# A row softmax on one core: the tail divides and stores ahead of the next maximum, and the whole-tile multiplies move to the even tiles

## The chip, the cores and the metric

One core of a Trainium2 chip runs the kernel. The metric is the device time of one execution in microseconds (us), lowest is best. A run's profile gives the span from the first to the last instruction; the device time is about 1.8 us longer.

## The reference

```python
# x: float32 (32, 512, 1024), temperature = 0.5
scaled = x / temperature
shifted = scaled - np.max(scaled, axis=-1, keepdims=True)
exp_x = np.exp(shifted)
return (exp_x / np.sum(exp_x, axis=-1, keepdims=True)).astype(np.float32)
```

There are 16,384 rows of 1,024 numbers, 67 MB in and 67 MB out.

## The kernel before

The rows are cut into 16 tiles (0 to 15) of 128 partitions with 8 rows each, 4 MB a tile. The kernel keeps six tile buffers (`BUFS`). The four outer tiles (0, 1, 14, 15) are worked in two groups of four rows, called 14a, 14b and so on below, the others in one group of eight.

```python
PASSES = [[4, 4]] * 2 + [[8]] * 12 + [[4, 4]] * 2
WHOLE = (3, 5, 7, 9, 11, 13)
ALIGNED = 3
BY_SP = 2
# ... cut: tiles, groups, dram() ...

def maximum(g):      # DVE: one reduction of the group, then bias = -scale * max
    ...
def exponential(g):  # ACT: one activation a row, exp(scale * x + bias), in place, with the row's sum
    ...
def divide(g):
    i, a, k = groups[g]
    _, sums, recip = small[g]
    nc.vector.reciprocal(recip, sums)
    if i in WHOLE:   # one multiplication for the tile
        xt = tiles[i][:, a : a + k, :]
        nc.vector.tensor_mul(xt, xt, recip.unsqueeze(2).to_broadcast([P, k, d]))
        return
    for b in range(k):  # or one a row
        nc.vector.tensor_scalar_mul(
            tiles[i][:, a + b, :], in0=tiles[i][:, a + b, :], scalar1=recip[:, b : b + 1]
        )

def store(g):        # when a tile's last group is divided; the next load waits for its buffer
    i, a, k = groups[g]
    if a + k == ROWS:
        queue = nc.scalar if i < len(PASSES) - BY_SP else nc.sync
        queue.dma_start(out=dram(of, i), in_=tiles[i])
        load()

for _ in range(BUFS):
    load()
for g in range(len(groups) + 1):
    if g < len(groups):
        maximum(g)
        exponential(g)
    if g > 0:
        divide(g - 1)
        store(g - 1)
    if g == ALIGNED:
        nc.vector.addr_align(128, offset=0, max_nops=0)
        nc.scalar.addr_align(128, offset=0, max_nops=0)
```

Loads go out on the queue of SyncE (SP), the stores of tiles 0 to 13 on that of ScalarE (ACT), those of 14 and 15 on SP's. In the trace they are the queues q1 and q10.

## Time and profile before

| | before |
|---|---|
| device time, first three runs | 318.0 us median (317.99 to 318.73) |
| span of the profiled run | 316.5 us |
| VectorE (DVE) busy | 250.8 us, 79% |
| ScalarE (ACT) busy | 148.2 us, 47% |
| moved by DMA | 134 MB, 433 GB/s from 40 to 280 us |

The page gives sums for the whole span, the windows view the same for chosen stretches, and the timeline the instructions in order, each with the idle time of its engine before it and what ended that in brackets. A DMA packet counts in the window of its start, so a share can be over 1 just behind a hole. The prediction below shows the lines that carry its argument. It also follows single packets: on a DMA engine that never pauses, each packet starts some 3 ns before the recorded end of the one in front, so one engine's packets can be followed through the trace, but for ties where two engines end within a nanosecond.

One more line of before is needed, from the view of everything that touches the output tensor (duration of issuing one in ns, then the times of the first and last issue): the stores on SP's queue.

```profile
L105 SPq DMA_DIRECT2D out_dram<-xt x2: 344/346/348, 291.4 to 303.6; - x2
```

### The profile page before, as it was taken

Reading aid. Unit: us, or ns where it says so; the run is one execution under the profiler, and the core shown is the slowest. Engines: PE = TensorE matmul, PEld = TensorE weight load, DVE = VectorE, ACT = ScalarE, POOL = GpSimd, SP = SyncE. Lnnn points to the kernel's source line nnn. Section 1 sums busy time; section 2 is a strip of 40 time slices with the busy share of each in tenths; the row PEclk is TensorE's granted clock in tenths of the full one; section 3 lists DMA queues with packets and bytes.
Section 4 is the critical chain, followed back from the end, with each engine's and each line's share of the span. In section 5 each row is a group of like instructions: output and inputs, shape, how many; then the busy total and the mean of one; then the engine's idle time right before and its main releaser. Section 6 shows DMA issues by size and latency. Waiting matters only on the chain.

```text
span 316.5 us, 534 instructions
## 1 busy us (share of the span) xinstructions
DVE 250.8 (79%) x146; ACT 148.2 (47%) x257; POOL 0.2 (0%) x4
## 2 busy tenths in 40 slices
DVE  0399999969989398994979859797697967999730
ACT  0176637681906429073380833709256092446600
POOL 0000000000000000000000000000000000000000
DMA  8999999999999999999999999999999999999996
GB/s 327 414 451 431 364 454 422 443 443 418 447 414 447 418 443 414 460 406 456 415 447 427 435 447 414 447 418 443 418 456 406 456 418 443 431 431 452 407 410 273
DMA packets 4613, 134.26 MB, mean 424 GB/s; under 512 B 512, under 2 KB 512, under 8 KB 512
## 3 DMA queue, kind: packets, MB, share of 16 engines
q1 hardware_dynamic: 2592, 75.50, 55.8%
q10 hardware_dynamic: 2016, 58.72, 43.0%
q14 instruction: 5, 0.04, 0.0%
HBM read 67.11 MB, written 67.11 MB: 424 GB/s over the span
## 4 chain that ended last, share of the span: by engine, by line
DVE 77%; another core or an unknown queue 11%; DMA 4%; ACT 3%; issue 1%; DVEq 0%; ACTq 0%
DVE top L70 43%; DVE xt L94 16%; DVE xt L97 16%; DMA xt<-in_x_dram 4%; ACT xt L79 3%; DVE recip L91 1%; DVE bias L73 1%; DVEq L154 0%; ACTq L154 0%
## 5 line engine op out<-in xcount | busy, mean ns | idle before, releaser
L79 ACT ACTIVATE xt<-xt,bias 128x1024 f32<-128x1024 f32 x128 | 145.2, 1135 | 139.2 <-DVE bias L73 121.8
L70 DVE TENSOR_REDUCE top<-xt 128x8 f32<-128x8192 f32 (+1 forms) x20 | 139.5, 6976 | 49.4 <-DMA xt<-in_x_dram 49.4
L97 DVE TENSOR_SCALAR xt<-xt,recip 128x1024 f32<-128x1024 f32 x80 | 54.3, 748 | 0.5
L94 DVE TENSOR_TENSOR xt<-xt,recip 128x8192 f32<-128x8192 f32 x6 | 52.1, 8692 | 0.2
L79 ACT ACTIVATION_READ_ACCUMULATOR xt<-xt,bias 128x1 f32 x128 | 23.8, 186 | 0.0
L79 ACT ACT_TABLE_LOAD x1 | 1.3, 1283 | 13.2 <-DMA xt<-in_x_dram 13.2
L91 DVE RECIPROCAL recip<-sums 128x8 f32<-128x8 f32 (+1 forms) x20 | 3.7, 185 | 2.0 <-ACT xt L79 2.0
L73 DVE TENSOR_SCALAR bias<-top 128x8 f32<-128x8 f32 (+1 forms) x20 | 3.4, 170 | 0.7
L140 POOL MEMSET const-bfloat16-1.0<- 128x1 bf16 x1 | 0.1, 101 | 0.0
L140 POOL MEMSET const-uint8-127<- 128x1 uint8 x1 | 0.1, 101 | 0.0
L140 POOL MEMSET const-float32-0.0<- 128x1 f32 x1 | 0.1, 98 | 0.2 <-issue 0.2
L140 POOL MEMSET const-float32-1.0<- 128x1 f32 x1 | 0.1, 98 | 0.0
## 6 DMA issues: line engine op xcount, KB each, us to landing
xt<-in_x_dram SPq DMA_DIRECT2D x16, 4096.0 KB, 50.4
out_dram<-xt ACTq DMA_DIRECT2D x14, 4096.0 KB, 28.8
out_dram<-xt SPq DMA_DIRECT2D x2, 4096.0 KB, 13.3
```

What stands on the lines that cost most here:

```text
L70: nc.vector.tensor_reduce(out=top, in_=tiles[i][:, a : a + k, :], axis=mybir.AxisListType.X, op=extreme)
L73: nc.vector.tensor_scalar_mul(bias, in0=top, scalar1=-scale)
L79: nc.scalar.activation(tiles[i][:, a + b, :], tiles[i][:, a + b, :], mybir.ActivationFunctionType.Exp, bias=bias[:, b : b + 1], scale=scal ...
L91: nc.vector.reciprocal(recip, sums)
L94: nc.vector.tensor_mul(xt, xt, recip.unsqueeze(2).to_broadcast([P, k, d]))
L97: nc.vector.tensor_scalar_mul(tiles[i][:, a + b, :], in0=tiles[i][:, a + b, :], scalar1=recip[:, b : b + 1])
L140: nc = _bacc.Bacc("TRN2", target_bir_lowering=False, num_devices=1)
```

## The change

Its intent: in the tail, where nothing is loaded any more, a tile should be divided and stored as soon as its exponentials are there, and not behind the maximum of the next tile. The other part turns the parity of the tiles that are multiplied whole (8.69 us instead of 5.39 in pieces), so that tile 13, the one ahead of the tail, is done in pieces.

```diff
-WHOLE = (3, 5, 7, 9, 11, 13)
+WHOLE = (2, 4, 6, 8, 10, 12)
 
 ALIGNED = 3
+
+ALONE = 14
@@
         for g in range(len(groups) + 1):
+
+            alone = g < len(groups) and groups[g][0] >= ALONE and groups[g][1] == 0
+            if g > 0 and alone:
+                divide(g - 1)
+                store(g - 1)
             if g < len(groups):
                 maximum(g)
                 exponential(g)
-            if g > 0:
+            if g > 0 and not alone:
                 divide(g - 1)
                 store(g - 1)
```

## The prediction

> **What bounds the kernel now.** I read the busy digits of the page first, then busy time by windows, then the waits, the timeline of VectorE (DVE) over the last 75 us, and last the single DMA packets of the trace. The page and the windows:
>
> ```profile
> DVE 250.8 (79%) x146; ACT 148.2 (47%) x257; POOL 0.2 (0%) x4
> ...
> DMA  8999999999999999999999999999999999999996
> ```
>
> ```profile
> core 0: us, DVE busy (x) ACT busy (x) POOL busy (x), PEclk, DMA share, GB/s
> ...
> 40.00:280.00 240.00, 202.83 (x99) 116.62 (x204) 0.00 (x0) 1.00 1.00 433
> 280.00:292.00 12.00, 11.86 (x15) 8.04 (x14) 0.00 (x0) 1.00 1.01 435
> 292.00:302.00 10.00, 8.05 (x10) 5.87 (x12) 0.00 (x0) 1.00 0.99 427
> 302.00:303.50 1.50, 1.50 (x3) 0.00 (x0) 0.00 (x0) 1.00 0.86 371
> 303.50:304.40 0.90, 0.10 (x1) 0.00 (x0) 0.00 (x0) 1.00 0.17 73
> ```
>
> The reader should see that DVE is idle for a fifth of the span, while the 16 DMA engines have share 1.00 and 433 GB/s from 40 to 280 us. Only one hole shows, at 303.5 to 304.4 us (share 0.17; a packet counts in the window of its start). So DMA is the bound, although the chain of waits puts 77% on DVE. The waits agree: it is DVE that waits for loads.
>
> ```profile
> DVE top L70 <- DMA xt<-in_x_dram: 49.4, 12, 13.2
> DVE recip L91 <- ACT xt L79: 2.0, 2, 1.8
> ```
>
> The tail of the timeline:
>
> ```profile
> 243.82 8.69 DVE L70 TENSOR_REDUCE top<-xt 128x8 f32<-128x8192 f32 x1 [1.63 <-DMA xt<-in_x_dram]
> ...
> 252.85 5.39 DVE L97 TENSOR_SCALAR xt<-xt,recip 128x1024 f32<-128x1024 f32 x8
> 263.19 4.42 DVE L70 TENSOR_REDUCE top<-xt 128x4 f32<-128x4096 f32 x1 [4.95 <-DMA xt<-in_x_dram]
> ...
> 267.95 8.69 DVE L94 TENSOR_TENSOR xt<-xt,recip 128x8192 f32<-128x8192 f32 x1
> 276.56 4.41 DVE L70 TENSOR_REDUCE top<-xt 128x4 f32<-128x4096 f32 x1
> ...
> 300.65 0.18 DVE L91 RECIPROCAL recip<-sums 128x4 f32<-128x4 f32 x1 [1.85 <-ACT xt L79]
> 300.86 2.74 DVE L97 TENSOR_SCALAR xt<-xt,recip 128x1024 f32<-128x1024 f32 x4
> ```
>
> Tile 13 was there from 243.8 us on, but its division waits behind the maximum of tile 14's first half, and that waits 4.95 us for load 14. In the timeline the store of tile 13 is issued at 276.7, of 14 at 291.4, of 15 at 303.6.
>
> The packets of the trace carry the verdict. Each of the 32 transfers is 128 packets of 32 KB, so 8 on each DMA engine, at 1.213 us each. An engine owes 256 packets, 310.5 us; the first starts at 1.76 us, so 312.3 us is the earliest end without any loss. The last packet ends at 315.26. At the seam between stores 14 and 15, twelve engines finish store 14 at 303.4 to 303.9 and stand still until 304.5, when the first packets of store 15 start there (0.84 us after its issue); averaged over 16 engines the hole costs 0.76 us. But two engines still have a packet of store 14 to do and finish it at 305.48 and 305.58; they pass into store 15 with no hole and end it at 315.16 and 315.26, the other fourteen at 314.2 to 314.4. So the end belongs to two late engines that never starve. They came late long before: around 35 us, when the first store starts, packets take 1.6 to 1.9 us, one 2.77, and without holes from there on nothing is made up.
>
> **What the Trainium skill says.** "HBM Reference", section "Specifications (TRN2)", says that a core streaming alone measures well above its share of the domain, about 425 GB/s, bounded by its 16 DMA engines; the 433 GB/s agree. "DMA: Bandwidth & Descriptors", section "Queues, rings and completion order", says that each DMA engine goes round-robin between the queues it has work for, packet by packet, and that sync's and scalar's queues lie on the same engines. The trace agrees: loads and stores each move about half of the 433. Thus a store that is issued earlier takes turns with the others and adds no bandwidth. The same page, section "Why a DMA increments its semaphore by 16 and not by 1", says that the engines of one DMA finish independently and only the full count means landed: hence the latest engine decides, as the ends at 314.2 and 315.26 show. "VectorE: DVE Perf Modes", section "The perf-mode tier table", has fp32 tensor_scalar at 2x and tensor_tensor at 1x; the trace has 5.39 us for a tile in eight pieces and 8.69 whole.
>
> **The change part by part.** (1) The parity. Six tiles are still multiplied whole, so DVE's sum stays 250.8 us. Stores of even tiles come up to 3.3 us (8.69 - 5.39) later, of odd ones earlier. In the middle DVE has 4.95 us to spare before each maximum after an eight-piece tile, and 1.6 after a whole one; with the parity turned these change places. The store queue doesn't run dry: store 1 ends its packets at 75.6, and store 2 goes from 66.2 to about 69.6. Only tile 2 pushes on DVE: its multiply ends at 60.8 + 8.7 = 69.5, not 66.2, while load 4 lands at 68.8, so the maximum of tile 4 starts 0.7 late, which the next slack of nearly 5 us takes up. Cost 0.
>
> (2) The tail, with durations from the timeline (maximum of 4 rows to its bias 4.44, four exponentials 4.6 until the sums are out, four multiplies 2.74, eight 5.39; some 0.2 from reciprocal to multiply). Tile 12, now whole: 252.85 + 8.69 = 261.54; its store goes from 258.3 to 261.6, behind store 11, which keeps that queue until 269.2. The exponentials of 13 end at 261.91, so its reciprocal at 261.95 and eight multiplies 262.2 to 267.6: store 13 at 267.6 instead of 276.7. Maximum 14a 267.5 to 271.9 (load 14 has been there since 263.2), exponentials to 276.8, maximum 14b beside them to 276.4, division 14a to 279.8. Now the second half must be divided ahead of maximum 15a, and DVE waits for the exponentials of 14b until 281.4 (1.6 us): division until 284.4, store 14 at 284.4 instead of 291.4. Maximum 15a from 284.3 (load 15 landed at 282.5), 15b from 288.8, exponentials of 15b until 298.2, last division 298.4 to 301.1: store 15 at 301.2 instead of 303.6. DVE's path gains 2.4 us: the 4.95 us wait for load 14 goes, about 0.4 of it comes back for 13's sums, and some 2 more for those of 14 and 15.
>
> (3) What becomes of that on DMA. Loads end at 280.9 as before. Store 12 keeps its queue until 285.3, 13 follows, 14 takes turns with 13 from about 286 on. All packets up to store 14 are the same work on engines that never pause, so it ends at about 303.5 on twelve engines, 305.6 on two, as before. Store 15 has packets ready at 301.2 + 0.84 = 302.0: the hole of 303.5 to 304.5 is closed. The twelve engines then end at 303.5 + 8 x 1.213 = 313.2, a microsecond sooner; the two late ones end at 305.58 + 9.70 = 315.28, as before. Sum: 2.4 us on DVE, 0.76 us of mean DMA idleness filled, near 0 at the end. From the last packet to the end of the span there are 1.2 us, and from span to time 1.8 (318.26 - 316.5); both stay.
>
> **The rivals.** First, the end follows the issue of store 15, as the chain of waits suggests: 318.0 - 2.4 = 315.6. Against it: between issue and end there is nothing for DMA to fill but the hole. Second, the late engines are chance of this profile, and others see the whole hole: 318.0 - 1.0 = 317.0. For it: one profile is one draw. Against it: the three timed runs are 317.99, 318.00 and 318.73. Without late engines the end would be 304.5 + 9.75 = 314.25, 1.0 us under the profiled one, about 317.25, and none of the runs is there. Third, a new wait makes it slower: late even stores empty the store queue, or tile 4's late maximum runs on to the end: at most +0.7, 318.7. Against it: 6 us of margin in the queue and the slack after tile 3. Fourth, instruction fetches (8 KB packets of 0.31 us on one engine, at 287 and 300 us) fall on the late engine: +0.3.
>
> **Range and chances.** I give six tenths to "late engines decide" (317.9), three tenths to the second rival or part of it (317.1), the rest to both sides: about 317.6 us. Range 316.5 to 318.6. Two per cent are 6.4 us; the largest gain that DMA allows is down to 312.3 + 1.2 + 1.8 = 315.3, 0.9%. So faster by over 2% has chance 0.01, within 0.98, slower 0.01.
>
> **What would show it.** Right: store 15 issued near 301.2, 14 near 284.4, 13 near 267.6; DMA share near 1 through 303 to 305 us; DVE's wait for loads down from 49.4 to about 44 (two of the twelve gone, 14's and 4's), its wait for ACT up from 2.0 to about 4.4; the last packets spread over 2 us, most at 313.2 and a few at about 315. Wrong: a last packet near 313.5 (the lateness isn't there or is made up), or a new hole before 300 us. An end above 319 us would mean that the store queue starved.

## The result, and the profile after

| | before | after |
|---|---|---|
| device time, median of 6 runs | 318.02 us (317.66 to 318.73) | 318.21 us (318.09 to 318.80) |
| span of the profiled run | 316.5 us | 316.3 us |
| last store issued | 303.6 us | 300.9 us |
| packets of 14 DMA engines end | 314.2 to 314.4 us | 313.0 to 313.6 us |
| packets of the two late ones end | 315.16, 315.26 us | 314.79, 315.07 us |

The ratio after to before is 1.0006, with a 95% interval from 0.9992 to 1.0019: the same time. Here and below a ratio is the mean time of one kernel's fast runs over that of the other's of the same rounds, so it is not quite the ratio of the quoted medians. For an experiment the other kernel is the kernel before.

The tail of DVE's timeline after the change:

```profile
252.69 8.69 DVE L96 TENSOR_TENSOR xt<-xt,recip 128x8192 f32<-128x8192 f32 x1
261.78 0.20 DVE L93 RECIPROCAL recip<-sums 128x8 f32<-128x8 f32 x1 [0.40 <-ACT xt L81]
262.02 5.39 DVE L99 TENSOR_SCALAR xt<-xt,recip 128x1024 f32<-128x1024 f32 x8
267.32 4.42 DVE L72 TENSOR_REDUCE top<-xt 128x4 f32<-128x4096 f32 x1
...
281.18 0.18 DVE L93 RECIPROCAL recip<-sums 128x4 f32<-128x4 f32 x1 [1.57 <-ACT xt L81]
281.39 2.74 DVE L99 TENSOR_SCALAR xt<-xt,recip 128x1024 f32<-128x1024 f32 x4
...
297.95 0.18 DVE L93 RECIPROCAL recip<-sums 128x4 f32<-128x4 f32 x1 [1.63 <-ACT xt L81]
298.17 2.74 DVE L99 TENSOR_SCALAR xt<-xt,recip 128x1024 f32<-128x1024 f32 x4
```

Tile 13 is now divided ahead of the maximum at 267.32, which finds its load in place: the 4.95 us wait is gone. In its stead stand short waits for ACT's sums, 0.40, 1.57 and 1.63 us. The waits view has them added up, and the output view the issues:

```profile
DVE top L72 <- DMA xt<-in_x_dram: 44.4, 10, 13.0
DVE recip L93 <- ACT xt L81: 4.1, 6, 1.6
```

```profile
L107 SPq DMA_DIRECT2D out_dram<-xt x2: 343/346/348, 284.2 to 300.9; - x2
```

The last division ends 2.7 us sooner than before and the last store is issued at 300.9 us. The windows show what the DMA engines make of it, first in the middle (433 GB/s, as before), then over the seam of the last two stores:

```profile
40.00:280.00 240.00, 206.66 (x105) 119.85 (x211) 0.00 (x0) 1.00 1.00 433
...
302.00:303.50 1.50, 0.00 (x0) 0.00 (x0) 0.00 (x0) 1.00 1.17 502
303.50:304.40 0.90, 0.00 (x0) 0.00 (x0) 0.00 (x0) 1.00 0.76 328
304.40:306.00 1.60, 0.00 (x0) 0.00 (x0) 0.00 (x0) 1.00 1.23 532
```

The share from 303.5 to 304.4 us was 0.17 before and is 0.76: the hole is closed. In the packets no engine is idle between 300 and 307 us (0.76 us on the mean engine before). Fourteen engines end 1.1 us sooner. The last packet ends 0.2 us sooner, and that is all that the span shows.

### The profile page after: what moved, and what is told of

It reads as the page before. It is cut to its first block, busy times and chain, and to the rows that moved or that the text cites. A ratio compares the mean times of both kernels' runs of the same rounds, so it can differ in the third digit from the quotient of the medians.

```text
span 316.3 us, 534 instructions
## 1 busy us (share of the span) xinstructions
DVE 251.0 (79%) x146; ACT 148.1 (47%) x257; POOL 0.2 (0%) x4
## 5 line engine op out<-in xcount | busy, mean ns | idle before, releaser
L72 DVE TENSOR_REDUCE top<-xt 128x8 f32<-128x8192 f32 (+1 forms) x20 | 139.5, 6976 | 44.4 <-DMA xt<-in_x_dram 44.4
```

Of the source, the lines that this page charges most:

```text
L72: nc.vector.tensor_reduce(out=top, in_=tiles[i][:, a : a + k, :], axis=mybir.AxisListType.X, op=extreme)
```

## The experiments

Twelve kernels ran; each was timed in five rounds against the kernel before on the same chip. Unless it says otherwise, an experiment starts from the changed kernel, whose time is 318.21 us.

### Which part of the change does anything?

**order_only**: the new order with the old parity.

```diff
-WHOLE = (2, 4, 6, 8, 10, 12)
+WHOLE = (3, 5, 7, 9, 11, 13)
```

> The order of the tail alone; tiles 3, 5 .. 13 stay the whole ones, so tile 13 takes 8.69 us and not 5.39 and the tail runs 3.3 us behind that of the changed kernel. All: the last store is issued near 204.2 + 100 = 304.2 us (changed kernel 300.94, before 303.63). Theory (the end is set by the two late DMA engines, which have work until 305.4 us whatever the order): the hole of the other engines is back, about 1.5 us long, and the time is as before, 318.0 to 318.4. Rival 1 (the end follows the issue of the last store): 3.3 us over the changed kernel, 321.5. Rival 2 (the two parts of the change each do something and cancel): off from 318.1 by 0.5 us or more, the other way than parity_only.

("204.2 + 100" is a slip of the pen for 304.2.) Measured: 318.52 us, ratio 1.0015 (1.0003 to 1.0028); last store issued at 303.9.

**parity_only**: the new parity with the old order.

```diff
-ALONE = 14
+ALONE = 99
```

> The parity alone; the maximum of tile 14 goes ahead of the division of 13 as before. All: tile 12 is multiplied until 261.4, the maximum of 14's first half starts at 263.0 when its load lands, that of 15 must wait about 1.8 us for its load (282.4), and the last store is issued near 302.0. Theory: the hole nearly closed, time as before, 318.0 to 318.3. Rival 1: 1.1 us over the changed kernel, 319.3. Rival 2: off from 318.1 by 0.5 us or more.

Measured: 318.35 us, ratio 1.0011 (0.9999 to 1.0024); last store at 302.3. The windows at the seam, order_only first:

```profile
303.50:304.40 0.90, 0.33 (x1) 0.00 (x0) 0.00 (x0) 1.00 0.18 73
```

```profile
303.50:304.40 0.90, 0.00 (x0) 0.00 (x0) 0.00 (x0) 1.00 0.59 255
```

With the order alone the hole is there (0.18), with the parity alone it is mostly closed (0.59), and the times differ by 0.2 us. The two parts don't cancel each other: neither is faster than before, though together they move the issue by 2.7 us. order_only is even slower than before by 0.1 to 0.9 us (its interval leaves out 1). Its last packet ends at 315.26 us as before, so its profile doesn't show where that comes from; it stays open. Rival 1, by which the end follows the issue, asked for 321.5 and 319.3.

### How late may the last store be?

**late1** and **late2**: one or two needless reductions of four rows ahead of the last division.

```diff
         for g in range(len(groups) + 1):
+            if g == len(groups):
+                for _ in range(1):      # late2: range(2)
+                    idle = stats.tile([P, 4], f32, name="idle")
+                    nc.vector.tensor_reduce(out=idle, in_=tiles[15][:, 0:4, :], axis=X, op=extreme)
```

> The changed kernel with one needless maximum of 4 rows (4.4 us of DVE) put in ahead of the last division; 1.6 of it fill the wait for the exponentials, so the last store is issued 2.8 us later, near 303.7. Theory: its packets are there at 304.6, the late engines are busy until 305.4, so the time stays: 318.2. Rival 1: 321.0.

> The same with two: 7.2 us later, issued near 308.1, packets from 309.0 on. Now no engine has anything left from 305.4 to 309.0, and theory says that the end moves by just that, 3.6 us, to 321.8. Rival 1: by 7.2, to 325.4. If the compute tail did not matter at all: 318.2.

Measured: late1 318.20 us (ratio 1.0005, 0.9993 to 1.0018) with the last store at 303.3; late2 321.56 us (ratio 1.0111, 1.0095 to 1.0126) with the last store at 308.1. The output view of both, then two windows of late2:

```profile
L107 SPq DMA_DIRECT2D out_dram<-xt x2: 343/346/348, 283.8 to 303.3; - x2
```

```profile
L107 SPq DMA_DIRECT2D out_dram<-xt x2: 343/346/348, 284.2 to 308.1; - x2
```

```profile
304.40:306.00 1.60, 1.56 (x4) 0.00 (x0) 0.00 (x0) 1.00 0.05 20
306.00:309.00 3.00, 2.03 (x4) 0.00 (x0) 0.00 (x0) 1.00 0.33 142
```

This is the verdict on the main question. 2.4 us of delay cost nothing, and 7.2 us cost 3.4: the end moves only by what exceeds the work that the last engine still has, until about 305.4 us. In late2 all engines run dry (share 0.05), and all 16 then end together, at 318.65 to 318.80. The late engines have lost their lateness there, because everybody waited for the same store.

### Is VectorE the bound in the middle?

**all_whole**: all of tiles 2 to 12 multiplied whole.

```diff
-WHOLE = (2, 4, 6, 8, 10, 12)
+WHOLE = tuple(range(2, 13))
```

> The changed kernel with all of tiles 2 to 12 multiplied whole, not every other one: five more tiles at 8.69 us instead of 5.39, so VectorE is busy 16.5 us more, 267.5 us. Theory (DMA engines are the bound in the middle, VectorE has 5 us to spare in every other tile): wait for loads down by 16.5 us, time 318.2. Rival (the chain of waits of before, which puts 77% on VectorE): up to 16 us more, 334.

Measured: 318.43 us, ratio 1.0010 (0.9998 to 1.0023). The busy line of the changed kernel's page, then that of all_whole, and its waits:

```profile
DVE 251.0 (79%) x146; ACT 148.1 (47%) x257; POOL 0.2 (0%) x4
```

```profile
DVE 267.4 (85%) x111; ACT 148.0 (47%) x257; POOL 0.2 (0%) x4
```

```profile
DVE top L72 <- DMA xt<-in_x_dram: 27.9, 10, 13.0
```

DVE has 16.4 us more to do and waits 16.5 us less for loads (44.4 - 27.9). This is how one sees that a busy engine at the head of the chain of waits is not the bound.

### Why are two engines late?

The prediction had put it down to the first store near 35 us. The trace of the changed kernel says otherwise when its two late engines are followed back from their last packets. All five fetches of instructions (8 KB packets of a queue of their own, 0.31 us each) lie on these two, at 43.2, 151.9 and 297.7 us on the one and 43.2 and 298.3 on the other. The packet behind a fetch took 0.17 to 0.54 us longer than the usual 1.213. With two slow packets more (94.8 and 114.2 us) that is 2.05 us on the one and 1.74 on the other, and they end 1.85 and 1.57 us behind the median engine (313.22). The slow packets at 33 to 42 us cost about 0.7 us on the mean of all 16: 0.66 and 0.67 on the two late ones, 0.52 to 0.86 on the other fourteen. So they make no engine later than the rest. The profile that the prediction read shows the same: followed back, the fetches at 286.9 and 300.0 us lie on its two late engines, one on each.

**few** takes away instructions. Its output is wrong, which doesn't matter for the time.

```diff
-        for b in range(k):
-            nc.scalar.activation(...row a + b..., bias=bias[:, b : b + 1], accum_out=sums[:, b : b + 1])
+        nc.scalar.activation(...rows a to a + k..., bias=bias[:, 0:1], accum_out=sums[:, 0:1])
@@
+        # reciprocal of sums[:, 0:1] alone; WHOLE as before with recip[:, 0:1] for all rows
-        for b in range(k):
-            nc.vector.tensor_scalar_mul(...row a + b..., scalar1=recip[:, b : b + 1])
+        nc.vector.tensor_scalar_mul(xt, in0=xt, scalar1=recip[:, 0:1])
```

> The changed kernel with as few instructions as its schedule allows: one exponential and one multiplication for a whole group, with the bias and the sum of the first of its rows, so the result is wrong on purpose; every transfer is unchanged. Theory as the traces so far suggest it (the two late engines are late because every fetch of instructions, 8 KB packets of 0.31 us, lands on the same two engines and also slows the packet behind it by 0.2 to 0.5): with some 200 instructions instead of 534 few or none of the five fetches are left, all 16 engines end within 0.8 us, the last packet ends near 313.4 and the time is 316.4. Rival (the lateness comes from the slow packets at the first store near 35 us, as the prediction said): last packet near 315, time 318.2.

Measured: 317.74 us, ratio 0.9975 (0.9962 to 0.9989). Faster than before, but by a third of what the fetch theory said. The line of the instruction queue on the page of the changed kernel, and then on that of few (packets, MB, share):

```profile
q14 instruction: 5, 0.04, 0.0%
```

```profile
q14 instruction: 2, 0.02, 0.0%
```

Two fetches are left, at 41.2 and 42.0 us. The last two engines end at 314.08 and 314.84, the median one at 313.36. So one of them is still 1.5 us late. The trace has more slow packets in this run (0.35 us at 96, 0.25 at 218 us) with no fetch ahead of them; ties between engines keep me from giving them all to one engine. Fewer fetches, sooner end: that held for the time, though not for the last packet of the profiled run (warm, below, has five fetches and ends at 314.84 too). That fetches alone make the lateness did not. The experiment also changes more than the fetches: its last store is issued at 299.4 us, not 300.9.

**align5** and **align4** move the aligned place in the instruction streams.

```diff
-ALIGNED = 3
+ALIGNED = 5      # align4: 4
```

> The changed kernel with its aligned place in the program behind group 5 and not 3. Fetch theory: the two early fetches (43 us) come later, near 80 us, and the two last ones (297.7 and 298.3 us) fall behind the end of the program and drop out; each late engine gains 0.5 to 0.7 us and the time is about 317.6. If the fetches only move, or others take their place: 318.2. Rival (first store): 318.2.

> The changed kernel with its aligned place behind group 4 and not 3 (align5 put a fetch at 66.6 us ahead of it, and its third one back in). Fetch theory: the two fetches of 298 us fall behind the end of the program and no other comes in: two fetches on the last engine, one on the other; last packet near 314.6 and not 315.1, time 317.8. If a third fetch comes in as in align5, or the fetch is not what counts: 318.2.

Measured: align5 318.35 us (ratio 1.0006, 0.9993 to 1.0018). The two fetches near 298 us went, but two came near 67 and 76 us where one had been at 43: four fetches before the end, at 65.0, 66.6, 75.5 and 190.0. One engine ends at 314.05, 0.7 sooner; the other at 315.19, no sooner. I had not foreseen the added fetch. align4 was made to avoid it: 317.58 us (317.49 to 318.04), ratio to before 0.9990 (0.9978 to 1.0003). Its page:

```profile
span 315.7 us, 534 instructions
...
q14 instruction: 3, 0.02, 0.0%
```

The two late engines carry those three fetches (57.7 and 170.8 us, and 54.1) and end at 314.18 and 314.08, 0.9 and 0.7 us sooner than in the changed kernel. Fetches and slow packets add up to 1.13 and 0.97 us on them, and they end 0.91 and 0.81 behind the median engine (313.27). It computes the same with the same instructions; only their addresses differ.

**nops** should have added fetches.

```diff
+            if 4 <= g <= 15:
+                for _ in range(43):
+                    nc.scalar.nop(nofuse=True)
```

> The changed kernel with 43 instructions that do nothing on ScalarE behind the exponentials of each of the groups 4 to 15, 516 in all; ScalarE is idle for half of the span, so they cost it nothing. [...]Fetch theory: four more fetches on the same late DMA engine, each 0.31 us and 0.1 to 0.5 more in the packet behind, together 2.2 us, and the whole of it shows at the end: 320.4 us, the last packet of that engine near 317.3 and the other engines as before near 313.2. Rival (what makes the engine late is something else): 318.2.

Measured: 318.16 us (318.04 to 318.60), ratio 1.0008 (0.9995 to 1.0020). The page still has 534 instructions and five fetches at the same times: as far as the profile shows, the empty instructions never reached the chip. So it tests nothing of the theory. It is of use as a second measurement of the changed kernel on the same chip as align4: there align4 is 0.58 us below it in the medians, and of five runs each the highest of align4 equals the lowest of nops.

**warm** asks whether the slow packets near 35 us are the price of the store queue's first use.

```diff
+        warm = stats.tile([P, 8], f32, name="warm")
+        nc.scalar.dma_start(out=warm, in_=xf[0:P, 0:8])
         for _ in range(BUFS):
             load()
```

> The changed kernel with a load of 4 KB on the scalar queue at the start, so that the first store near 33 us is not that queue's first transfer. The packets between 34 and 38 us took up to 0.75 us longer than the 1.213 of all others, 0.7 us in all on each engine. If that is the price of the queue's first use, it now falls on the start and the time is 317.5; if it is the price of the first write among reads, nothing changes: 318.2.

Measured: 318.20 us, ratio 0.9997 (0.9984 to 1.0009). The packets from 33 to 42 us cost 0.88 us on the mean engine, not less than the 0.70 of the changed kernel. First use isn't it; what it is stays open. In this trace too, the last two engines (314.84 and 314.69) are those with three and two fetches.

### Taking work from the late engines

**shift8** and **relieve** wanted to shift bytes of the last store between engines. The page that both expectations speak of is the Trainium skill's "DMA: Bandwidth & Descriptors", section "Why a DMA increments its semaphore by 16 and not by 1": a transfer issued from sync or scalar runs on k of the 16 engines, the lowest-numbered ones, with k the largest number up to 16 that divides the outermost sizes of both sides. The traces agree on the k: they hold one 4-byte packet for each engine of each transfer, and one more (513 with 32 transfers on 16 engines), and in shift8 there are 529, in relieve 657, as 8 and 7 engines for the small ones ask. Which engines these are, they don't show.

```diff
-            queue.dma_start(out=dram(of, i), in_=tiles[i])
+            # shift8, last tile: three transfers of the partitions 0-111, 112-119, 120-127
+            for lo, hi in ((0, 112), (112, 120), (120, 128)) if i == len(PASSES) - 1 else ((0, P),):
+                queue.dma_start(out=dram(of, i)[lo:hi], in_=tiles[i][lo:hi])
```

> The changed kernel with the last store in three transfers, of 112, 8 and 8 partitions. If transfers are dealt out over the DMA engines as the skill's page says, the first gives each engine 7 packets and the others one each to the lower eight engines alone: 9 packets for eight engines, 7 for eight, and not 8 for all. Theory: where both late engines are among the eight that get less, they end near 313.9, the others near 314.5, and the time is 317.6; where one is among those that get more, it ends 1.2 us later and the time is 319.4. If no single engine decides but the sum of the work: 318.2.

```diff
+            # relieve, last tile: rows 0-6 and half of row 7 as before, the other half of row 7:
+            for j in range(18):
+                queue.dma_start(out=o[j:126:18, ROWS - 1, h:], in_=t[j:126:18, ROWS - 1, h:])
+            queue.dma_start(out=o[126:128, ROWS - 1, h:], in_=t[126:128, ROWS - 1, h:])
```

> The changed kernel; of the last store, half of the eighth row (2 KB of 32 on each partition) goes in transfers of 7 partitions, 18 apart, so that they lie on different ports, which as the skill's page has it run on the seven lowest engines alone. Each engine sheds 0.6 us; the lowest seven get 1.35 on top. Theory: if both late engines are above the seventh they end 0.6 us earlier, the others near 314, and the time is 317.6; if a late one is among the seven it ends 0.75 us later, 319.0. If small transfers cost more than their bytes (as in shift8), the seven end later than 315 and the time is over 318.5; then the trace still shows whether the late engines are among them.

Both miss what they were for. shift8 took 323.13 us (ratio 1.0155, 1.0141 to 1.0169): the packets of the small transfers took up to 4.4 us instead of 1.213. A window of its end:

```profile
312.00:321.50 9.50, 0.00 (x0) 0.00 (x0) 0.00 (x0) 1.00 0.31 69
```

69 GB/s: half a megabyte in some 8 us. The Trainium skill, "SBUF — State Buffer", section "Door 1: The DMA port swizzle", says that a transfer's rate depends on how many of the memory's 16 ports its partitions reach; by its table these 16 partitions lie on four. That fits in kind, and I had overlooked it; no run was made to test it. (In relieve, where the partitions of a small transfer lie 18 apart, its 2 KB packets took 0.12 us at most, against 0.084 in the large transfer.) relieve took 327.83 us (ratio 1.0309, 1.0295 to 1.0323), because the small transfers were issued so slowly:

```profile
301.27 22.23 SPq L114 DMA_DIRECT2D out_dram<-xt  x18
```

Eighteen transfers of 14 KB took 22 us to issue: one every 0.74 us for most, and a standstill of 7.7 us between the sixth and the seventh. It ended at 314.6 us, when the latest engines had done the 28 KB packets of the large transfer and were working off the 2 KB packets behind them. So it may be a wait for these and not a cost of issuing; that is not shown. One thing can be kept: the two engines that finish the large transfer last (313.58 and 314.16 us) went on with packets of the seven-partition transfers, so both are among the seven engines that these transfers use. Moving bytes onto these was the wrong direction in any case.

## Why the prediction was right, and where not

- *The end belongs to the late DMA engines, and the order of the tail is off the path*: right, and shown. The times stayed within 0.4 us of each other while the issue of the last store lay anywhere from 300.9 to 303.9 us (changed kernel, parity_only, late1, order_only), and moved by 3.4 us when it passed what the late engines can take up (late2: 3.6 foretold).
- *The new schedule of DVE*: right within 0.4 us at each store (13 at 267.4 against 267.6, 14 at 284.2 against 284.4, 15 at 300.9 against 301.2), as were the waits for loads (44.4 against 44) and for ACT (4.1 against 4.4).
- *The hole closes, fourteen engines end a microsecond sooner*: right. 313.0 to 313.6 stand against 313.2, and the last packet ended at 315.07 against 315.28.
- *No cost in the middle from the parity*: right; all_whole shows that even 16 us of DVE work there change nothing that is clear of noise.
- *The number*: 318.21 lies in the range, but 0.6 us above the middle of it. Part of that is arithmetic: its own sum, 315.28 + 1.2 + 1.8, gives 318.3, and it set "late engines decide" at 317.9 without saying why. The other part was mis-sized by choice: three tenths went to a lateness that comes by chance, with an end near 317.1. All six runs are at 318.09 or above, and the late engines are there in every trace in which DMA isn't made to wait.
- *"They came late long before: around 35 us, when the first store starts"*: this step failed. The slow packets there fall on all engines (0.66 and 0.67 us on the late ones of the changed kernel, 0.52 to 0.86 on the others). What the two late engines alone carry are the fetches of instructions and slow packets near them; align4, with two fetches fewer, ends the last packet 0.9 us sooner. The fourth rival had the fetches as a small extra of 0.3 us, not as the cause, and took them for something that might still come; in the profile before, those two fetches lay on the late engines already. That the changed kernel, with its new program, again had three fetches on one engine and two on another was luck as far as the prediction goes: it didn't ask where they would fall, and in align4 another place went with 0.6 us less (against nops, on the same chip). How much of the lateness is due to them is not settled: in few, one engine stayed 1.5 us late with at most two fetches in the trace.

A version below both kernels is align4, at 317.58 us. The gain is 0.4 to 0.6 us, its interval against before just includes 1, and it was not tried on the order of before, so what part the change has in it is open.

## What to carry to other kernels

When DMA never pauses, look for the last packet of each single DMA engine before you shorten the compute tail: here a sooner store only filled holes of the engines that had them, and the latest engine set the end. Test it by delaying the store: if some microseconds of delay are free, issuing it sooner is worth nothing. Even the fetching of instructions is traffic on these engines; another place of it went with 0.6 us here.

## What the Trainium skill lacked or had wrong

- "Runtime: NRT & Kernel Launch", section "Instruction fetch mechanics", speaks of refills in 16 KiB blocks, mostly hidden. Here each fetch is one 8 KB packet of 0.31 us. All fetches of the changed kernel lie on the same two of the 16 DMA engines, and the data packet behind one took 0.17 to 0.54 us longer. With DMA as the bound that is not hidden: two fetches fewer (align4) went with a last packet 0.9 us sooner, 314.18 and not 315.07.
- "DMA: Bandwidth & Descriptors" has no cost of issuing a transfer whose partitions lie apart: on SP's queue issuing such a transfer of 7 partitions, 18 apart, took 0.70 us for most where one of 4 MB took 0.34 (in shift8, with 8 adjoining partitions, 0.38 and 1.49), and eighteen of them took 22.23 us, a standstill of 7.7 us among them. Whether it is the spacing that costs, no run shows.
- No page that I read has the slow-down at the first store among loads: packets between 33 and 42 us took longer, by 0.6 to 0.9 us in all on the mean engine in every trace looked at; a transfer on the same queue before it did not take it away.
